# First mixer of an encoder: shifted copies from SBUF to SBUF on two queues, taps of the last tiles spread differently, the gate half normalised first, idle products round the statistics

## The chip, the cores and the metric

The kernel runs on one core of one Trainium2 chip. The metric is the device time of one execution in microseconds (us); the median of several runs counts. Engines are named as in the profile: PE is TensorE (matmuls; PEld its weight loads), DVE is VectorE, ACT is ScalarE, POOL is GpSimd, SP is SyncE, which only issues DMAs here. ACTq and SPq are the DMA queues of ACT and SP.

## The reference, cut to what matters

Two encoder layers on 256 positions of 2048 channels, in float32. Each has a mixer and a feed-forward part with a convolution. The change touches the first mixer alone:

```python
def _conformer_conv(h, w_in, b_in, dw_w, dw_b, ln_g, ln_b, w_out, b_out):
    u = h @ w_in + b_in
    a, gate = jnp.split(u, 2, axis=-1)
    u = a * jax.nn.sigmoid(gate)
    u = _causal_dwconv(u, dw_w, dw_b)
    u = jax.nn.silu(_layernorm(u, ln_g, ln_b))
    return u @ w_out + b_out
```

Here `h` is the RMS norm of the input, `_causal_dwconv` sums 31 shifted copies of a channel with a weight for each (31 taps), and `_layernorm` takes mean and variance over the 2048 channels of a position. The second mixer is an attention, and it, the feed-forward parts and the final norm stay as they are.

## The kernel before

Channels lie on the partitions, 128 at a time, positions along the free axis (S = 256). KT = 16 tiles of 128 channels make up the 2048. Weights come in pieces of 128x1024: SP loads `raw`, ACT rounds it to `hi` (L150), POOL or DVE takes the rest as `lo` (L152), and PE multiplies hi and lo parts. Five raw and six hi and lo buffers go round.

In the first mixer a loop runs over the 16 tiles. Tile i's product with w_in (L229) has 96 matmuls in four steps of 24, in groups of two products with `hi` and one with `lo`; both halves, `a` and gate, stand in one PSUM tile `pp`. `post(i)` then multiplies by the norm's factor `rstd` (L453, DVE), takes the sigmoid `G` of the gate half (L455, ACT) and writes the product into `cpad`, one of three padded tiles (L457, DVE). The convolution of tile i is split in two. Of its 31 taps the first 4·G[i] are done on PE: `u` is written to DRAM (`ud`, L469), read back four times, shifted by one position each time, into the four quarters of a tile `R` (L473, all on ACT's queue), and `taps` multiplies R by diagonals `dg` that POOL builds (L482). A tap product (L498) is 32 columns wide, one of four column groups. G is 3 for tiles 0 to 12 (12 products each), 5 for tile 13 and 6 for tile 14. The other taps are done one after the other on DVE (L536), spread through the steps by `tap_step`. The last tile has no time for copies: 18 taps on PE with full diagonals (`last_taps`, L507; POOL builds them ahead in tiles Y and A, L489) and 13 on DVE in two chains that take turns (L515 to L519).

`dev` adds the bias and takes off a shift `mp`; sums over the tiles of the value and of its square are kept on POOL (L582, L583) and folded into two tiles M at tile 14 (L591). The layernorm sums over the partitions on PE (L286), makes mean and factor in a short chain of DVE and POOL (`mom`, L611 to L617), spreads them over the partitions with four rows products (L292), normalises, and starts w_out (L238, L239).

The order of each engine is set when the kernel is built: a scheduler puts instructions where its own cost model expects their inputs, so a change in one place can move others. `self.at(n, f)` runs `f` n steps later.

Of the kernel before, what the change touches and what calls it, by code (L numbers as in the profile page):

```python
# [8 lines left out]
F32 = mybir.dt.float32  # L9
F32R = mybir.dt.float32r  # L10
AF = mybir.ActivationFunctionType
ALU = mybir.AluOpType
AX = mybir.AxisListType
ET = mybir.EngineType
P = 128
S = 256
EPS = 1e-6
HD = 64
CK = 31
# [6 lines left out]
class Cfg:  # L26


    def __init__(self, d, f, kc=4):
        self.D, self.F = d, f  # L30
        self.KT = d // P
        self.FT = f // P
        self.H = d // (2 * HD)
        self.KC = kc
        self.NW = kc * 256
        self.kcs = [(i, kc) for i in range(0, self.KT, kc)]
        full = self.KT // 2
        first = self.FT % full or full
        self.chunks = [(0, first)] + [(i, full) for i in range(first, self.FT, full)]
        self.VK = kc // 2  # L40
        self.NA, self.NB = self.KT + self.KT // 2 + 1, 8

        self.G = [3] * (self.KT - 3) + [5, 6, 0]

        self.ND = 18

    def dsub(self, ci):
        k0, n = self.chunks[ci]
# [13 lines left out]
class Builder:  # L62
# [379 lines left out]
    def conv_module(self, nin, nout):  # L442
        c, a = self.c, self.a
        nc = self.nc
        KT = c.KT
        D, hh, st = {}, {}, {}
        UW = S + CK + 1

        def post(i, ps):
            with self.tc.high_priority():  # L450

                t = ps[:, :, 0:S]
                nc.vector.tensor_tensor(t, t, nin["rstd"].unsqueeze(1).to_broadcast([P, 2, S]), ALU.mult)  # L453
                sg = self.b1("G")
                nc.scalar.activation(sg, t[:, 1, :], AF.Sigmoid, bias=self.col("bin", KT + i))  # L455
                u = self.cpad[i % 3]
                nc.vector.scalar_tensor_tensor(u[:, CK - 1:CK - 1 + S], t[:, 0, :], self.col("bin", i), sg, ALU.add,  # L457
                                               ALU.mult)
                if i == KT - 1:
                    nc.scalar.activation(self.c2(), sg[:, 0:2], AF.Silu)  # L460
            gm = max(c.G)
            if i == KT - 1:
                self.at(0, lambda: last_taps(u, dgl))
                return

            g = c.G[i]
            n = 4 * (g - 1) + S
            ud = self.dr.tile([P, UW], F32, tag="ud", name=self.nm("ud"), bufs=2)
            nc.scalar.dma_start(ud, u)  # L469
            R = self.ph1.tile([P, 4, 4 * (gm - 1) + S], F32, tag="R", name=self.nm("R"), bufs=2)  # L470
            udv = ud.rearrange("(j c) n -> c j n", j=4)
            for s in range(4):
                nc.scalar.dma_start(R[s * 32:(s + 1) * 32, :, :n], udv[:, :, s:s + n])  # L473
            dg = self.ph1.tile([P, 4 * gm, 32], F32, tag="dg", name=self.nm("dg"))[:, :4 * g, :]

            queue = self.tc.issue_after(self.pool_lo) if i == 0 else ExitStack()
            with queue:
                diagonals(i, g, dg)
            self.at(5 if i < KT - 2 else 4, lambda: taps(i, u, R, dg))

        def diagonals(i, g, dg):
            nc.gpsimd.tensor_tensor(dg, self.cmask.unsqueeze(1).to_broadcast([P, 4 * g, 32]),  # L482
# [10 lines left out]
        def taps(i, u, R, dg):  # L493
            g = c.G[i]
            acc = self.psx("t" if i % 3 == 2 else "s", [P, S])
            for gp in range(g):
                for j in range(4):
                    nc.tensor.matmul(acc[j * 32:(j + 1) * 32, :], dg[:, 4 * gp + j, :], R[:, j, 4 * gp:4 * gp + S],  # L498
                                     start=(gp == 0), stop=(gp == g - 1), tile_position=(0, 32 * j))
            chains.append([i, u, acc, list(range(4 * g, CK))])  # L500

        def last_taps(u, dgl):

            i = KT - 1
            acc = self.psx("s", [P, S])
            for j, w in enumerate(dgl):
                nc.tensor.matmul(acc, w, u[:, j:j + S], start=(j == 0), stop=(j == len(dgl) - 1))  # L507
            while chains:
                tap_step(1000)
            pt = self.pp.tile([P, 2, 512], F32, tag="pp", name=self.nm("pp"))  # L510
            part = [pt[:, x, :S] for x in range(2)]
            for n, j in enumerate(range(len(dgl), CK)):
                w, p = self.col("cw", i * CK + j), part[n % 2]
                if n == 0:
                    nc.vector.scalar_tensor_tensor(p, u[:, j:j + S], w, st["mp"], ALU.mult, ALU.subtract)  # L515
                elif n == 1:
                    nc.vector.tensor_scalar(p, u[:, j:j + S], w, self.col("cb", i), ALU.mult, ALU.add)
                else:
                    nc.vector.scalar_tensor_tensor(p, u[:, j:j + S], w, p, ALU.mult, ALU.add)  # L519
            self.flush()  # L520
            e = self.b1("O")
            nc.scalar.copy(e, acc)
            nc.vector.tensor_tensor(e, part[0], e, ALU.add)
            dev(i, part[1], e)

        dgl = []
        chains = []
# [73 lines left out]
        def layernorm():  # L601
            self.flush()
            while chains:
                tap_step(1000)
                self.flush()
            self.every = None
            self.free(nin["xh"].values())
            mom = self.sm.tile([P, 2, 2], F32, tag="mom", name="mom", bufs=1)
            v, rc, mr = self.c2(), self.c2(), self.c2()
            late = st["late"].rearrange("p (a b) -> p a b", b=2)[:, :, 0]  # L610
            nc.vector.scalar_tensor_tensor(mom.rearrange("p a b -> p (a b)"), late, 1.0 / c.D, st["early"], ALU.mult,  # L611
                                           ALU.add)
            mean, ex2 = mom[:, 0, :], mom[:, 1, :]
            nc.vector.scalar_tensor_tensor(v, mean, -1.0, mean, ALU.mult, ALU.mult)
            nc.vector.scalar_tensor_tensor(v, v, EPS, ex2, ALU.add, ALU.add)
            nc.gpsimd.tensor_tensor(rc, v, self.mhalf, ALU.pow)
            nc.vector.tensor_tensor(mr, mean, rc, ALU.mult)  # L617

            rp = [self.psx("s", [P, S]) for _ in range(2)]
            rs = self.b2("E")  # L620
            for x, v in enumerate((rc, mr)):
                self.rows(rp[x], v)
            pools = [pr for pr in range(2, KT // 2) if pr % 2 == 0]
            ops = (ALU.mult, ALU.subtract)

            def norm(pr, part, j=None):
                d = D[pr][1]
                if j is not None:
                    nc.vector.tensor_tensor(d[:, j, :], d[:, j, :], rp[part], ops[part])
                elif pr in pools:  # L630
                    nc.gpsimd.tensor_tensor(d, d, rs[:, part, :].unsqueeze(1).to_broadcast([P, 2, S]), ops[part])
                else:
                    nc.vector.tensor_tensor(d, d, rp[part].unsqueeze(1).to_broadcast([P, 2, S]), ops[part])

            def act(i):
                z = self.psx("to"[i % 2], [P, S])
                nc.scalar.activation(z, D[i // 2][1][:, i % 2, :], AF.Silu, scale=self.col("lng", i),
                                     bias=self.col("lnb", i))
                hh[i] = self.act_tile()
                nc.scalar.copy(hh[i][1][:, 0, :], z)  # L640
                return z

            def low(i, z):
                h = hh[i][1]
                nc.vector.tensor_tensor(h[:, 1, :], z, h[:, 0, :].bitcast(F32), ALU.subtract)  # L645

            with self.tc.manual_schedule(engines={ET.DVE, ET.Activation, ET.Pool}):
                for j in range(2):
                    norm(0, 0, j)
                    norm(0, 1, j)  # L650
                for x in range(2):
                    nc.scalar.copy(rs[:, x, :], rp[x])
                for pr in pools:
                    norm(pr, 0)
                    norm(pr, 1)
                todo = [(pr, part) for pr in range(1, KT // 2) if pr not in pools for part in range(2)]
                for i in range(KT):
                    z = act(i)
                    for _ in range(2 if i == 1 else 1 if i > 1 else 0):
                        if todo:  # L660
                            norm(*todo.pop(0))
                    low(i, z)
            self.free(D.values())
            self.free([st["sd"]])
# [403 lines left out]
```

## Time and profile before

| | us |
|---|---|
| median of 3 runs | 2267.56 |
| lowest and highest run | 2267.46, 2270.97 |
| the profiled execution | 2268.81 |
| its span in the trace | 2267.0 |
| PE busy | 2219.3 |
| DVE busy | 1635.4 |
| ACT busy | 1205.2 |
| POOL busy | 292.0 |

All times of rows are from the one profiled execution, from the start of its span. The first mixer ends at about 270 us. A time behind an arrow in brackets is the idle time of the engine before the row, and what ended it. A group "x24" is 24 records; a tap product and a ones product have two records each.

### The profile page before, as it was taken

Reading aid. Unit: us, or ns where it says so; the run is one execution under the profiler, and the core shown is the slowest. Engines: PE = TensorE matmul, PEld = TensorE weight load, DVE = VectorE, ACT = ScalarE, POOL = GpSimd, SP = SyncE. Lnnn points to the kernel's source line nnn. Section 1 sums busy time; section 2 is a strip of 40 time slices with the busy share of each in tenths; the row PEclk is TensorE's granted clock in tenths of the full one; section 3 lists DMA queues with packets and bytes.
Section 4 is the critical chain, followed back from the end, with each engine's and each line's share of the span. In section 5 each row is a group of like instructions: output and inputs, shape, how many; then the busy total and the mean of one; then the engine's idle time right before and its main releaser. Section 6 shows DMA issues by size and latency. Waiting matters only on the chain.

```text
span 2267.0 us, 34768 instructions
## 1 busy us (share of the span) xinstructions
PE 2219.3 (98%) x13382; PEld 1944.0 (86%) x13382; DVE 1635.4 (72%) x2491; ACT 1205.2 (53%) x1788; POOL 292.0 (13%) x197
## 2 busy tenths in 40 slices
PE   5999899999999999999999999999999999999998
PEld 5999788788888888888888888888888888888887
DVE  4788675877767777677777677767777677676774
ACT  4333554655545555555555555555555455554554
POOL 4788510100000000000110101110000000000002
PEclk8999999999999999999999999999999999999999
DMA  6677357755555555555555545455555555555552
GB/s 234 196 215 212 116 192 161 241 185 193 187 191 188 187 186 189 191 187 186 195 167 167 167 161 168 151 196 185 189 186 187 192 187 187 191 187 188 188 189 98
DMA packets 126007, 417.55 MB, mean 184 GB/s; under 512 B 14416, under 2 KB 26704, under 8 KB 125840
## 3 DMA queue, kind: packets, MB, share of 16 engines
q1 hardware_dynamic: 113040, 400.42, 53.9%
q10 hardware_dynamic: 11520, 11.45, 2.0%
q0 software_dynamic: 1280, 3.46, 1.3%
q8 instruction: 105, 1.72, 0.3%
q14 instruction: 62, 0.51, 0.1%
HBM read 407.55 MB, written 7.72 MB: 183 GB/s over the span
## 4 chain that ended last, share of the span: by engine, by line
PE 94%; DMA 2%; DVE 1%; POOL 0%; ACT 0%; issue 0%; ACTq 0%; POOLq 0%; DVEq 0%
PE pp L238 48%; PE pp L239 25%; PE pp L229 7%; PE pp L236 4%; PE pp L235 2%; PE pp L807 1%; PE pp L809 1%; PE pp L808 1%; DMA raw<-in_w_up_dram 1%; PE s L498 1%; DMA R<-ud 0%; PE o L292 0%; PE s L854 0%; DMA ud<-cpad 0%; PE t L498 0%; PE o L286 0%
## 5 line engine op out<-in xcount | busy, mean ns | idle before, releaser
L238 PE MATMUL pp<-act,hi 128*128 128x512 f32 x3902 | 1382.6, 396 | 6.2 <-DVE act L645 3.1
L239 PE MATMUL pp<-act,lo 128*128 128x256 f32 x3902 | 1097.5, 281 | 0.0
L150 ACT CAST hi<-raw 128x1024 fp32r<-128x1024 f32 x752 | 788.0, 1049 | 529.2 <-PE pp L238 180.9
L152 DVE TENSOR_TENSOR lo<-raw,hi 128x1024 fp32r<-128x1024 f32 x686 | 846.0, 1234 | 301.0 <-ACT hi L150 299.0
L238 PEld LDWEIGHTS pp<-act,hi 128*128 128x128 f32 x3902 | 733.8, 188 | 167.4 <-DVE act L645 3.4
L239 PEld LDWEIGHTS pp<-act,lo 128*128 128x128 f32 x3902 | 741.1, 190 | 10.3
L238 PE MATMUL pp<-actb,hi 128*128 128x512 f32 x856 | 306.8, 396 | 1.7 <-ACT hi L150 1.7
L239 PE MATMUL pp<-actb,lo 128*128 128x256 f32 x856 | 240.8, 281 | 0.8 <-DVE lo L152 0.8
L333 POOL TENSOR_TENSOR ssq<-ssq,Z 128x512 f32<-128x512 f32 x24 | 35.6, 1483 | 1516.6 <-ACT Z L329 1516.5
L229 PE MATMUL pp<-act,hi 128*128 128x256 f32 x1088 | 203.4, 289 | 9.1 <-ACT act L279 6.2
L238 PEld LDWEIGHTS pp<-actb,hi 128*128 128x128 f32 x856 | 160.7, 188 | 40.1 <-ACT hi L150 2.0
L229 PEld LDWEIGHTS pp<-act,hi 128*128 128x128 f32 x1088 | 173.7, 196 | 15.6 <-ACT act L279 6.2
L152 POOL TENSOR_TENSOR lo<-raw,hi 128x1024 fp32r<-128x1024 f32 x66 | 158.3, 2414 | 57.6 <-ACT hi L150 52.1
L239 PEld LDWEIGHTS pp<-actb,lo 128*128 128x128 f32 x856 | 162.0, 189 | 1.3 <-DVE lo L152 1.1
L229 PE MATMUL pp<-act,lo 128*128 128x256 f32 x544 | 156.5, 288 | 1.7 <-POOL lo L152 1.5
L382 ACT COPY E<-pp 128x512 f32<-128x512 f32 x109 | 63.9, 586 | 171.5 <-PE pp L236 163.8
L268 DVE TENSOR_TENSOR E<-pp,E 128x512 f32<-128x512 f32 x104 | 71.8, 691 | 105.1 <-ACT E L266 104.9
L266 ACT COPY E<-pp 128x512 f32<-128x512 f32 x104 | 60.8, 585 | 162.7 <-PE pp L236 162.5
L704 DVE SCALAR_TENSOR_TENSOR Y<-fpad,prm,Y 128x256 f32<-128x256 f32 x352 | 146.8, 477 | 0.0
L384 DVE TENSOR_TENSOR x<-pp,x 128x512 f32<-128x512 f32 x101 | 69.7, 690 | 89.5 <-ACT E L382 89.0
L701 ACT ACTIVATE Y<-fpad,prm 128x256 f32<-128x256 f32 x176 | 96.3, 595 | 47.5 <-DVE fpad L697 47.5
L229 PEld LDWEIGHTS pp<-act,lo 128*128 128x128 f32 x544 | 106.7, 196 | 2.1 <-POOL lo L152 1.7
(222 smaller groups left out, 1841.9 us busy)
## 6 DMA issues: line engine op xcount, KB each, us to landing
raw<-in_w_up_dram SPq DMA_DIRECT2D x352, 512.0 KB, 3.9
raw<-in_w_down_dram SPq DMA_DIRECT2D x176, 512.0 KB, 3.9
raw<-in_w_in_dram SPq DMA_DIRECT2D x64, 512.0 KB, 4.4
raw<-in_w_qk_dram SPq DMA_DIRECT2D x64, 512.0 KB, 3.6
raw<-in_w_out_dram SPq DMA_DIRECT2D x32, 512.0 KB, 3.9
raw<-in_w_v_dram SPq DMA_DIRECT2D x32, 512.0 KB, 3.6
raw<-in_w_o_dram SPq DMA_DIRECT2D x32, 512.0 KB, 3.6
R<-ud ACTq DMA_DIRECT2D x52, 132.0 KB, 4.6
```

The costliest lines, as they stand in the source:

```text
L150: nc.scalar.copy(hi[:, :n], raw[:, :n])
L152: ins = eng.tensor_tensor(lo[:, :n], raw[:, :n], hi[:, :n].bitcast(F32), ALU.subtract)
L229: nc.tensor.matmul(ps[:, 0:S], w[:, kk, cs], xt[:, x, :], start=(k == first and n == 0), stop=(k == last and n == 2))
L236: nc.tensor.matmul(*main, start=False, stop=True)
L238: nc.tensor.matmul(*main, start=(k == first), stop=False)
L239: nc.tensor.matmul(*corr, start=False, stop=False)
L266: nc.scalar.copy(cs, ps[:, :, S:])
L268: nc.vector.tensor_tensor(t, ps[:, :, 0:S], cs, ALU.add)
L382: nc.scalar.copy(cs, ps[:, :, S:])
L384: nc.vector.tensor_tensor(x, ps[:, :, 0:S], x, ALU.add)
L701: nc.scalar.activation(y[:, j, :], u[:, j, FK - 1:], AF.Identity, scale=self.col("fw", ch * FK + FK - 1), bias=self.col("fb", ch))
L704: nc.vector.scalar_tensor_tensor(y[:, j, :], u[:, j, q:q + S], self.col("fw", ch * FK + q), y[:, j, :], ALU.mult, ALU.add)
```

## The change

The copies of `u` into R go from SBUF to SBUF with no DRAM tile between: sixteen DMAs of 32 partitions for each tile, eight on SP's queue and eight on ACT's, instead of one write and four reads on ACT's. Of tile 14's taps, the seven of DVE no longer stand in the common chain: `few_taps` computes them into a tile of their own one step after `post`, and `taps` of tile 14 comes one step earlier. The last tile has 16 taps on PE instead of 18, so no A diagonals, and 15 on DVE. Tile 15's gate half is multiplied by `rstd` ahead of the other half. In the layernorm PE gets idle products (ones by ones, 128x128, nobody reads the result): seven ahead of the rows products and eight behind them.

```diff
-        self.ND = 18
+        self.ND = 16
...
-                nc.vector.tensor_tensor(t, t, nin["rstd"].unsqueeze(1).to_broadcast([P, 2, S]), ALU.mult)
+                if i < KT - 1:
+                    nc.vector.tensor_tensor(t, t, nin["rstd"].unsqueeze(1).to_broadcast([P, 2, S]), ALU.mult)
+                else:
+                    for x in (1, 0):
+                        nc.vector.tensor_tensor(t[:, x, :], t[:, x, :], nin["rstd"], ALU.mult)
...
-            ud = self.dr.tile([P, UW], F32, tag="ud", name=self.nm("ud"), bufs=2)
-            nc.scalar.dma_start(ud, u)
             R = self.ph1.tile([P, 4, 4 * (gm - 1) + S], F32, tag="R", name=self.nm("R"), bufs=2)
-            udv = ud.rearrange("(j c) n -> c j n", j=4)
-            for s in range(4):
-                nc.scalar.dma_start(R[s * 32:(s + 1) * 32, :, :n], udv[:, :, s:s + n])
+            for j in range(4):
+                for s in range(4):
+                    (nc.sync if s < 2 else nc.scalar).dma_start(R[s * 32:(s + 1) * 32, j, :n], u[j * 32:(j + 1) * 32, s:s + n])
...
-            self.at(5 if i < KT - 2 else 4, lambda: taps(i, u, R, dg))
+            if i == KT - 2:
+                self.at(1, lambda: few_taps(i, u))
+            self.at(5 if i < KT - 2 else 3, lambda: taps(i, u, R, dg))
...
-            chains.append([i, u, acc, list(range(4 * g, CK))])
+            if i < KT - 2:
+                chains.append([i, u, acc, list(range(4 * g, CK))])
+            else:
+                self.at(1, lambda: dev(i, acc, part14[0]))
+
+        part14 = []
+
+        def few_taps(i, u):
+
+            p = self.psx("o", [P, S])
+            for n, j in enumerate(range(4 * c.G[i], CK)):
+                w = self.col("cw", i * CK + j)
+                if n == 0:
+                    nc.vector.scalar_tensor_tensor(p, u[:, j:j + S], w, st["mp"], ALU.mult, ALU.subtract)
+                else:
+                    nc.vector.scalar_tensor_tensor(p, u[:, j:j + S], w, p, ALU.mult, ALU.add)
+            e = self.b1("O")
+            nc.scalar.activation(e, p, AF.Identity, bias=self.col("cb", i))
+            part14.append(e)
...
             e = self.b1("O")
-            nc.scalar.copy(e, acc)
-            nc.vector.tensor_tensor(e, part[0], e, ALU.add)
-            dev(i, part[1], e)
+            nc.scalar.copy(e, part[0])
+            nc.vector.tensor_tensor(e, part[1], e, ALU.add)
+            dev(i, acc, e)
...
+            idle = self.pp.tile([P, 2, 512], F32, tag="pp", name=self.nm("pp"))
+
+            def keep_warm(n):
+                for _ in range(n):
+                    i = nc.tensor.matmul(idle[:, 0, :P], self.ones, self.ones, start=True, stop=True)
+                    self.tc.keep_in_program_order(i)
+
+            keep_warm(7)
             mom = self.sm.tile([P, 2, 2], F32, tag="mom", name="mom", bufs=1)
...
                 self.rows(rp[x], v)
+            keep_warm(8)
```

The scheduler also moves other instructions. On PE, in the middle of tile 10's product (`pp`), where its first step gives way to the second, stand the taps of tile 8 (into `t`). Before:

```order
L229 MATMUL pp_1892<-act_138,hi_1720 128x256 x2
L229 MATMUL pp_1892<-act_138,lo_1721 128x256
L498 MATMUL t_1917<-R_1711,dg_1716 32x256 x12
L229 MATMUL pp_1892<-act_145,hi_1772 128x256 x2
L229 MATMUL pp_1892<-act_145,lo_1773 128x256
```

On PE, the same place after the change:

```order
L229 MATMUL pp_1990<-act_138,hi_1808 128x256 x2
L229 MATMUL pp_1990<-act_138,lo_1809 128x256
L502 MATMUL t_2015<-R_1787,dg_1804 32x256
L229 MATMUL pp_1990<-act_145,hi_1860 128x256 x2
L502 MATMUL t_2015<-R_1787,dg_1804 32x256 x9
L229 MATMUL pp_1990<-act_145,lo_1861 128x256
```

The twelve tap products stood in one run; now nine do, and three stand alone ahead of it among the w_in products, one of them here and two further up.

On ACT, round the sigmoid of an early tile (`G`: G_681 is tile 2's before; G_699 is tile 2's and G_883 tile 3's after the change), with the casts of the weights and the copies. Before:

```order
L150 CAST hi_615<-raw_454 128x1024
L150 CAST hi_651<-raw_484 128x1024
L150 CAST hi_695<-raw_527 128x1024
L150 CAST hi_747<-raw_577 128x1024
L455 ACTIVATE G_681<-pp_533,prm 128x256
L469 DMA ud_684<-cpad_258 128x288
L150 CAST hi_789<-raw_613 128x1024
L473 DMA R_686<-ud_684 32x4x264 x4
```

On ACT after the change (hi_723 is the first weight piece of tile 4's product):

```order
L459 ACTIVATE G_699<-pp_551,prm 128x256
L475 DMA R_526<-cpad_255 32x264 x3
L150 CAST hi_633<-raw_462 128x1024
L150 CAST hi_669<-raw_492 128x1024
L475 DMA R_702<-cpad_258 32x264 x8
L459 ACTIVATE G_883<-pp_727,prm 128x256
L150 CAST hi_723<-raw_545 128x1024
L570 ACTIVATE M_765<-s_576,prm 128x256
L150 CAST hi_775<-raw_595 128x1024
```

Casts that stood ahead of a sigmoid now stand behind it, and behind copies.

On POOL, the end of the mixer (`lo` pieces, the sums L582 and L583, the folds M). Before:

```order
L152 TENSOR_TENSOR lo_2868<-raw_2691,hi_2867 128x1024
L152 TENSOR_TENSOR lo_3116<-raw_2735,hi_3115 128x1024
L582 TENSOR_TENSOR act_914<-act_914,act_2787 128x512
L583 TENSOR_TENSOR lnsq<-lnsq,Z_2861 128x512
L152 TENSOR_TENSOR lo_3139<-raw_2795,hi_3138 128x1024
L591 TENSOR_TENSOR M_2971<-act_914 128x256
L591 TENSOR_TENSOR M_2972<-lnsq 128x256
```

On POOL after the change, whose last `lo` pieces are the ninth and those before it from tile 14's sigmoid on:

```order
L152 TENSOR_TENSOR lo_2956<-raw_2757,hi_2955 128x1024
L152 TENSOR_TENSOR lo_2991<-raw_2793,hi_2990 128x1024
L152 TENSOR_TENSOR lo_3051<-raw_2829,hi_3050 128x1024
L613 TENSOR_TENSOR M_3083<-act_952 128x256
L605 TENSOR_TENSOR lnsq<-lnsq,Z_3044 128x512
L152 TENSOR_TENSOR lo_3284<-raw_2883,hi_3283 128x1024
L152 TENSOR_TENSOR lo_3307<-raw_2953,hi_3306 128x1024
L613 TENSOR_TENSOR M_3084<-lnsq 128x256
```

The second fold stands behind two more `lo` pieces, and the sum of squares behind the first fold.

## Rows read from the trace of the kernel before

**Rows 1.** the page, busy time of an engine, share of the span, instructions
```profile
PE 2219.3 (98%) x13382; PEld 1944.0 (86%) x13382; DVE 1635.4 (72%) x2491; ACT 1205.2 (53%) x1788; POOL 292.0 (13%) x197
```

**Rows 2.** the chain of waits, 176 to 200 us: start, length, what
```profile
177.41 1.43 PE s L498 x24
178.84 11.71 PE pp L229 x96
```

**Rows 3.** PE's timeline, taps of tiles 12 and 13 among w_in products
```profile
216.55 0.28 PE L229 MATMUL pp<-act,lo 128*128 128x256 f32 x1
216.76 1.50 PE L498 MATMUL s<-R,dg 128*32 128x256 f32 x24
...
218.53 0.29 PE L229 MATMUL pp<-act,lo 128*128 128x256 f32 x1
...
229.69 0.28 PE L229 MATMUL pp<-act,lo 128*128 128x256 f32 x1
229.90 2.37 PE L498 MATMUL s<-R,dg 128*32 128x256 f32 x40
...
232.53 0.28 PE L229 MATMUL pp<-act,lo 128*128 128x256 f32 x1
```

**Rows 4.** PE's timeline, the ones product among w_in products
```profile
80.05 0.28 PE L229 MATMUL pp<-act,lo 128*128 128x256 f32 x1
80.17 0.59 PE L556 MATMUL o<-M,ones 128*128 128x256 f32 x2
...
80.83 0.28 PE L229 MATMUL pp<-act,lo 128*128 128x256 f32 x1
```

**Rows 5.** PE's timeline, tile 0's taps
```profile
61.54 1.50 PE L498 MATMUL s<-R,dg 128*32 128x256 f32 x24 [1.16 <-DMA R<-ud]
```

**Rows 6.** PE's timeline, rows products and the first w_out product
```profile
257.36 1.66 PE L292 MATMUL s<-ident,c 128*128 128x128 f32 x8 [1.52 <-POOL c L616]
262.11 0.80 PE L238 MATMUL pp<-act,hi 128*128 128x512 f32 x1 [3.09 <-DVE act L645]
```

**Rows 7.** POOL's timeline
```profile
35.69 0.61 POOL L489 TENSOR_TENSOR A<-ident,cprm 128x256 f32<-128x256 f32 x1
...
224.25 9.47 POOL L152 TENSOR_TENSOR lo<-raw,hi 128x1024 fp32r<-128x1024 f32 x4
...
241.64 1.28 POOL L582 TENSOR_TENSOR act<-act,act 128x512 f32<-128x512 f32 x1
...
247.30 0.72 POOL L591 TENSOR_TENSOR M<-lnsq 128x256 f32<-128x256 f32 x1
```

**Rows 8.** the tile R, its DMAs
```profile
DMA to landing us min/median/max: 2.4/4.7/7.2
```

**Rows 9.** timelines of DVE and ACT, from tile 14's normalisation to mom
```profile
227.13 0.70 DVE L453 TENSOR_TENSOR pp<-pp,rstd 128x512 f32<-128x512 f32 x1 [0.96 <-PE pp L229]
...
228.00 0.47 ACT L455 ACTIVATE G<-pp,prm 128x256 f32<-128x256 f32 x1
...
233.87 1.77 ACTq L473 DMA_DIRECT2D R<-ud  x4
...
254.24 0.42 DVE L569 TENSOR_TENSOR act<-pp,O 128x256 f32<-128x256 f32 x1
255.95 0.16 DVE L611 SCALAR_TENSOR_TENSOR mom<-o,early 128x4 f32<-128x4 f32 x1 [1.29 <-PE o L286]
```

**Rows 10.** groups by line, 56 to 262 us: busy, mean ns, idle before
```profile
L150 ACT CAST hi<-raw 128x1024 fp32r<-128x1024 f32 x56 | 58.5, 1048 | 117.2 <-PE pp L229 54.5 <-DMA R<-ud 31.4 <-POOL dg L482 11.3
```

**Rows 11.** windows of 2 us: busy (x) of PE, PEld, DVE, ACT, POOL; PEclk; DMA
```profile
256.00:258.00 2.00, 0.64 (x5) 0.64 (x6) 0.66 (x5) 0.00 (x0) 0.72 (x1) 0.96 0.00 0
258.00:260.00 2.00, 1.02 (x5) 0.72 (x4) 1.33 (x4) 0.11 (x1) 0.00 (x0) 0.50 0.00 0
266.00:268.00 2.00, 2.00 (x8) 1.71 (x7) 2.00 (x5) 1.94 (x6) 1.92 (x2) 0.50 0.00 0
268.00:270.00 2.00, 2.00 (x13) 1.78 (x12) 1.47 (x4) 1.39 (x4) 0.16 (x1) 0.98 0.01 4
```

## The prediction

> **What bounds the kernel now.** I read the page first: TensorE (PE) is busy for 98% of the span [rows 1]. So an operation added on PE costs its own length unless PE was idle there, and work taken from another engine is worth only the PE idle time that it ended. The change lies in the first mixer, up to about 270 us. There the chain of waits shows the rhythm of a tile: 96 products of w_in in 11.71 us, 0.122 each, then one run of tap products [rows 2]. No step of another engine stands in that part of the chain. The timeline of PE then gives prices: what a run of tap products adds between two w_in products [rows 3], and what a single full-precision product adds [rows 4]. Last I looked for places where PE does stand: before tile 0's taps (1.16 us, for a DMA into R) [rows 5] and round the layernorm, where the first rows product waits for POOL and the first w_out product 3.09 us for DVE [rows 6].
>
> **The price of a tap product, and of a run.** The run of tile 12 is 12 products in three rounds of four column groups (24 records); from the lo product before it to the one behind it 218.53 − 216.55 = 1.98 us pass. One step of the usual rhythm is three products, 0.36, so the run adds 1.62. Tile 13's run of 20, in five rounds, adds 232.53 − 229.69 − 0.36 = 2.48 [rows 3]. Two rounds more cost 0.86, so a round is 0.43 and each run has 0.33 besides, whatever its length. Check: 96 × 0.122 + 1.62 = 13.3, and the chain has 1.43 + 11.71 = 13.1 for a tile [rows 2].
>
> **Lone tap products: +23.6.** The order of PE after the change splits the taps. Each tile of 0 to 12 keeps a main run of 9 to 11 products, and one to three products are issued before it in short runs of their own, among w_in products; up to the end of tile 14's product I count 44 runs where there were 13, so 31 more, 28 of them a single product and 3 of two or three. A short run fills one round at most. It takes what a round takes, 0.43, and the fixed 0.33 of a run: 0.76. The main run keeps three rounds, since the fullest column group still has three products, so nothing is given back. 31 × 0.76 = 23.6. No row shows a 32-column product alone, so I bound it. From below, the nearest row is the ones product: lo to lo 80.83 − 80.05 − 0.36 = 0.42 [rows 4], hence 31 × 0.42 = 13.0. Nearer to none, as if it ran beside the w_in products, is a rival below. From above, 0.76. I take the upper one, because the fixed part appears in both tap runs that I measured and not at the ones product, which has the width of its neighbours.
>
> The 0.33 per run and the ones product's 0.42, the same as one round without it, suggest that going from 128 columns to 32 and back is what costs. The Trainium skill, "TensorEngine Tiling (Array Packing)", section Tiling Modes (Key Properties), says that changing the tiling mode, not just the tile, drains TensorE. By that rule every lone product would pay two such changes and the sum above would stand; without it the term would be 13.0.
>
> **Gone at the start: −0.6 and −1.2.** ND goes from 18 to 16, so the A diagonals (0.61 on POOL) no longer stand ahead of the lo pieces and rc [rows 7]: −0.6, or 0 if rc waits for something else. Tile 0's copies no longer go through DRAM; the PE wait of 1.16 before its taps [rows 5] goes, unless the sixteen copies take as long: R's copies land 2.4 to 7.2 us after issue [rows 8], and ACT needs 0.44 to issue one (four in 1.77) [rows 9]. Eight issues are 3.5; with the median landing of 4.7 that is 8.2, near what two transfers one after the other take. I take −1.2, at worst 0.
>
> **ACT's order at tile 4: +2.8, and the copies of tile 3: +1.0.** Before, ACT's casts run four ahead of a tile's sigmoid. After, the first cast of tile 4's weights stands behind tile 3's sigmoid, and that waits for tile 3's last product and the normalisation. From the norm's start to the sigmoid 228.00 − 227.13 = 0.87, the sigmoid 0.47 [rows 9], the cast 1.05 [rows 10], and some 0.2 from product to norm: 2.6 after the product's end. PE has only tile 2's taps, 1.62, to bridge: it stands 1.0. Its third product then needs the lo piece, which POOL makes in 9.47/4 = 2.37 [rows 7], while PE has two products (0.24) and a ones product (0.42): 1.8 more. Together 2.8; 0 if the scheduler's order leaves time that I do not see. Tile 3's eight copies on ACT stand behind four casts: 4 × 1.05 + 3.5 + 2.4 landing = 10.1 us after the sigmoid, of a tile of 13.1, while lone products of these taps are due ahead of their main run. I take 1.0, with 0 to 4 as bounds.
>
> **The end, from tile 14's sigmoid (228.00, called G): 0.0 (−2.9 to +3.1).** Before, POOL's last sum M<-lnsq ends at 247.30 + 0.72, G + 20.0, and mom on DVE starts at 255.95, G + 28.0, 1.71 after the last add of tile 15's deviation starts [rows 7, 9]: DVE's tap chain was last. After, POOL has nine lo pieces, two sums of 1.28 and two of 0.72 from the cast behind G on: G + 0.47 + 1.05 + 9 × 2.37 + 2.56 + 1.44 = G + 26.9. With the same 1.71 behind it mom is at G + 28.6: +0.6. DVE's chain gets shorter (tile 14's taps, which alternated with it, have their own place earlier), but that is worth nothing once POOL is last; so are the gate half first and the wait before tile 14's taps. Seven idle products then stand ahead of the rows products. The four rows products (8 records) take 1.66 [rows 6], 0.41 each, at a granted clock of 0.50, the 1.2 GHz level, and the clock is 0.96 to 258 us [rows 11]: seven idle products take 1.5 at the full 2.4 GHz and 2.9 at half. Before, the rows products started 257.36 − 255.95 = 1.41 behind mom, so +0.1 to +1.5: +0.8. Eight more stand behind, 1.7 to 3.3, in a gap that is 4.75 from rows to w_out with 1.66 of it used: +0.1. In return the clock: from 262.11 on the w_out products run at 0.50 until 268 (0.98 from there) [rows 6, 11]; if PE kept the full level, these 5.9 us would be 2.95, a gain of up to 2.9. I take half, −1.5, since PE still has an idle stretch before w_out. +0.6 + 0.8 + 0.1 − 1.5 = 0.0.
>
> **Sum.** 23.6 − 0.6 − 1.2 + 2.8 + 1.0 + 0.0 = +25.6. The profiled execution took 2268.8, 1.2 above the median of the runs, so against the median 2293.
>
> On the copies: the Trainium skill, "DMA: Bandwidth & Descriptors", Rules for kernel authors, says that spreading DMAs over several issuers adds no bandwidth, since all run on the same 16 engines, and saves only issue time. By it, sixteen small copies among raw weight loads would not land faster than four large ones did; that is the case of late copies below.
>
> **Rivals.**
> Lone products at 0.42 each: a full-precision product and no fixed part. For it, the ones product; against it, the width does change. 13.0 + 2.0 = +15.0: 2282.6.
> Copies late: sixteen DMAs per tile wait on SP behind raw loads whose buffers come free late, and PE stands at lone products which come earlier than the run did. For it, landing up to 7.2 [rows 8]; against it, the taps have had some 13 us. A quarter of a microsecond at half of the 44 runs and 4 at tile 3 would make about +10: 2303.
> Not slower: a lone product hides beside the w_in products, as one column group does beside another (a quarter round, 0.11, taken out of the main run). Then the 31 runs cost nothing, the rest is +2.0: 2269.6, no change. It decides below 2.5/31 = 0.08 per lone product. Against it stands the 0.33 that no run escaped.
> Faster: that, tile 4's wait and tile 3's copies hidden (−3.8), the whole clock gain (−1.4 more) and the idle products at the full clock (−0.7): 2.0 − 5.9 = −3.9, 2263.7. Even all of them only come to the edge of 0.2%.
> The redistribution does nothing: earlier taps of tile 14, ND, and the gate half only move what ends before POOL's last sum; that is inside my forecast.
>
> **How the numbers follow.** A run of this kernel tells from no change about 0.2%, 4.5 us. Forecast 0.58 (its own range 2287 to 2299), lone products at 0.42: 0.17, copies late: 0.14, not slower: 0.08, faster: 0.03. The likeliest is 2293. The low end takes the second case with the terms at their low bounds (13.0 − 0.6 − 1.2 − 2.9 + 2.8 = 11.1): 2278.6, so 2278; the high end lies past the late copies, 2306. Slower 0.89, same 0.08, faster 0.03.
>
> **What would show it.** Lone records of the tap line among w_in products, with lo-to-lo distances of 1.1 us instead of 0.36 (0.78 in the second case); a tile of about 15 us instead of 13.1; PE idle at the first product of tile 4 for ACT's cast; rc about 0.6 earlier; POOL's M<-lnsq ending last before mom; rows at 0.5 or 1.0 clock behind the idle products. Everything behind the first mixer should be shifted, not changed. I am wrong if tiles still last 13.1, or if PE waits for R at many places.

## The result, and the profile after

The changed kernel takes 2296.62 us (median of 4 runs, 2296.17 to 2299.18), the kernel before 2267.86 (4 runs): a ratio of 1.0126 with a 95% interval of 1.0109 to 1.0144. It is 29 us slower. The forecast was 2293, with 2278 to 2306 for its range.

The page of the changed kernel, against [rows 1]: the span is 28.1 longer and PE is busy for 29.0 more, with 26 more records: 30 of the fifteen idle products, less 4 of the two diagonals that went.

```profile
span 2295.1 us, 35125 instructions
...
PE 2248.3 (98%) x13408; PEld 1953.1 (85%) x13408; DVE 1638.2 (71%) x2494; ACT 1202.7 (52%) x1789; POOL 290.8 (13%) x196
```

Four marks cut the 28.1 into pieces: tile 14's sigmoid G, mom, the first w_out product, the end of the span.

| piece | before | after | difference | forecast |
|---|---|---|---|---|
| to tile 14's sigmoid | 228.00 | 251.88 | +23.9 | +25.6 |
| sigmoid to mom | 27.95 | 32.93 | +5.0 | +0.6 |
| mom to the first w_out product | 6.16 | 7.55 | +1.4 | +0.9 |
| first w_out product to the end | 2004.89 | 2002.74 | −2.15 | −1.5 |

**The short runs.** PE's timeline of the changed kernel, round a single tap product (two records) among w_in products; to be read against [rows 3, 4]:

```profile
58.09 0.28 PE L229 MATMUL pp<-act,lo 128*128 128x256 f32 x1
58.21 0.28 PE L229 MATMUL pp<-act,hi 128*128 128x256 f32 x1
58.42 0.62 PE L502 MATMUL s<-R,dg 128*32 128x256 f32 x2
58.97 0.38 PE L229 MATMUL pp<-act,hi 128*128 128x256 f32 x1
59.19 0.28 PE L229 MATMUL pp<-act,lo 128*128 128x256 f32 x1
```

From lo to lo 59.19 − 58.09 = 1.10 us pass where a step takes 0.36, so the short run costs 0.74; the forecast had 0.76. The reader is to see that the tap record starts 0.21 behind the record ahead of it, and that the next w_in product starts 0.55 behind it: in between no w_in product starts. Measured from the start of the record ahead of a run to that of the second one behind it, less two usual distances (0.24), every short run in the trace costs 0.74 or 0.75, those of two and three products too, and the main runs of 9 and 10 still cost 1.60 to 1.61, as the runs of 12 did before (1.62). 31 × 0.74 = 22.9.

**Tile 4.** PE's timeline where tile 4's product begins:

```profile
84.99 1.50 PE L502 MATMUL t<-R,dg 128*32 128x256 f32 x22
87.29 0.50 PE L229 MATMUL pp<-act,hi 128*128 128x256 f32 x2 [0.81 <-ACT hi L150]
87.67 0.70 PE L578 MATMUL o<-M,ones 128*128 128x256 f32 x2
89.73 0.39 PE L229 MATMUL pp<-act,lo 128*128 128x256 f32 x1 [1.36 <-POOL lo L152]
```

The run of tile 2's taps ends, PE waits 0.81 for ACT's cast, does two products and the ones product, and waits 1.36 for POOL's lo piece: 2.2 for the 2.8 that were forecast. The wait of 1.16 before tile 0's taps [rows 5] is gone. 22.9 + 2.2 − 1.2 and the 0.5 by which rc comes earlier make 23.4 of the 23.9. The 1.0 for tile 3's late copies is not there: no wait of PE in the mixer is for R.

**The end.** ACT's timeline of the changed kernel, from tile 14's sigmoid:

```profile
251.88 0.47 ACT L459 ACTIVATE G<-pp,prm 128x256 f32<-128x256 f32 x1 [11.83 <-DVE pp L454]
252.25 1.99 ACT L150 CAST hi<-raw 128x1024 fp32r<-128x1024 f32 x2
253.71 0.52 ACTq L475 DMA_DIRECT2D R<-cpad  x1
254.13 1.05 ACT L150 CAST hi<-raw 128x1024 fp32r<-128x1024 f32 x1
254.26 7.34 ACTq L475 DMA_DIRECT2D R<-cpad  x7
261.70 1.05 ACT L150 CAST hi<-raw 128x1024 fp32r<-128x1024 f32 x1 [6.52 <-DMA R<-cpad]
```

and POOL's, which waits for these casts:

```profile
253.37 7.27 POOL L152 TENSOR_TENSOR lo<-raw,hi 128x1024 fp32r<-128x1024 f32 x3 [5.75 <-ACT hi L150]
262.83 2.41 POOL L152 TENSOR_TENSOR lo<-raw,hi 128x1024 fp32r<-128x1024 f32 x1 [2.19 <-ACT hi L150]
...
280.32 0.71 POOL L613 TENSOR_TENSOR M<-lnsq 128x256 f32<-128x256 f32 x1
```

The casts go on behind the sigmoid, then the eight copies of R take ACT's queue for 7.9 us, and the fourth cast comes only at 261.70, behind the copies. POOL's lo piece starts 2.19 late at 262.83, and its last fold ends at 280.32 + 0.71 = 281.03, G + 29.2 instead of the forecast G + 26.9. DVE adds the last part to it (`M<-M,O`). PE sums the result over the partitions (L286), ACT scales the sums into `early`, and mom on DVE follows:

```profile
281.07 0.43 DVE L614 TENSOR_TENSOR M<-M,O 128x256 f32<-128x256 f32 x1 [2.38 <-POOL M L613]
...
282.60 0.17 ACT L617 ACTIVATE early<-o 128x4 f32<-128x4 f32 x1 [3.46 <-PE o L286]
...
284.81 0.16 DVE L642 SCALAR_TENSOR_TENSOR mom<-o,early 128x4 f32<-128x4 f32 x1 [3.32 <-PE o L286]
```

PE has nothing to do meanwhile. Its timeline shows the wait, the sums, the idle products (L635), the rows products (L292), and w_out:

```profile
281.55 1.02 PE L286 MATMUL o<-ones,M 128*128 128x2 f32 x4 [4.98 <-DVE M L614]
282.83 1.02 PE L286 MATMUL o<-ones,act 128*128 128x2 f32 x4 [0.26 <-ACT early L617]
283.70 0.99 PE L286 MATMUL o<-ones,O 128*128 128x2 f32 x4
284.56 3.33 PE L635 MATMUL pp<-ones 128*128 128x128 f32 x14
287.68 1.55 PE L292 MATMUL s<-ident,c 128*128 128x128 f32 x8
289.07 1.95 PE L635 MATMUL pp<-ones 128*128 128x128 f32 x16
292.36 0.50 PE L238 MATMUL pp<-act,hi 128*128 128x512 f32 x1 [1.34 <-DVE act L677]
```

and windows of 2 us the clock, as in [rows 11]:

```profile
278.00:280.00 2.00, 0.00 (x0) 0.00 (x0) 0.58 (x2) 0.42 (x1) 2.00 (x2) 0.62 0.45 127
280.00:282.00 2.00, 0.45 (x3) 0.46 (x3) 0.43 (x1) 0.00 (x0) 1.70 (x3) 0.50 0.66 182
290.00:292.00 2.00, 1.02 (x10) 0.83 (x8) 0.60 (x3) 1.74 (x5) 1.32 (x2) 1.00 0.00 0
292.00:294.00 2.00, 1.64 (x8) 1.22 (x8) 1.97 (x5) 1.03 (x3) 2.00 (x2) 1.00 0.01 4
```

PE waits 4.98 us, its granted clock goes to 0.50 (the 1.2 GHz level) while it waits, and the sums, the seven idle products and most of the rows products run before it is back. From POOL's fold to mom 3.8 us pass instead of the 1.71 that were forecast. Before, the last sums ran at the full clock:

```profile
254.81 0.58 PE L286 MATMUL o<-ones,act 128*128 128x2 f32 x4 [0.78 <-DVE act L569]
255.25 0.59 PE L286 MATMUL o<-ones,O 128*128 128x2 f32 x4
```

These two groups took 1.03 us then (254.81 to 255.84) and take 1.86 now (282.83 to 284.69). The rest of the difference is a longer way: before, the sums of M and `early` were done ahead of the last add; now both stand behind the fold, 1.33 us from the end of DVE's add (281.50) to the sums of `act` (282.83). At 290 us the clock is 1.00 and w_out starts at it, where before it started at 0.50.

### The profile page after: what moved, and what is told of

It is laid out like the page before. It is cut to its first block, busy times and chain, and to the rows that moved or that the text cites. A ratio compares the mean times of both kernels' runs of the same rounds, so it can differ in the third digit from the quotient of the medians.

```text
span 2295.1 us, 35125 instructions
## 1 busy us (share of the span) xinstructions
PE 2248.3 (98%) x13408; PEld 1953.1 (85%) x13408; DVE 1638.2 (71%) x2494; ACT 1202.7 (52%) x1789; POOL 290.8 (13%) x196
## 4 chain that ended last, share of the span: by engine, by line
PE 94%; DMA 2%; POOL 1%; DVE 1%; issue 1%; ACT 0%; POOLq 0%; SPq 0%; DVEq 0%; ACTq 0%
PE pp L238 47%; PE pp L239 24%; PE pp L229 7%; PE pp L236 4%; PE pp L235 2%; PE pp L839 1%; PE pp L841 1%; PE pp L840 1%; DMA raw<-in_w_up_dram 1%; PE s L502 1%; POOL lo L152 1%; DMA raw<-in_w_in_dram 0%; PE o L286 0%; PE o L292 0%; PE t L502 0%
```

## The experiments

Ratios are to the kernel before on the same chip. Theory A is the forecast: a short run costs 0.74 on PE, wherever it stands.

**Split alone** (e6_split_alone). The kernel before; the first tap product of tiles 1 to 12 is issued one step earlier, and the products of a tile's taps are pinned in their order (the functions that do it are left out here):

```diff
-            self.at(5 if i < KT - 2 else 4, lambda: taps(i, u, R, dg))
+            if 0 < i < KT - 3:
+                self.at(4, lambda: first_tap(i, R, dg))
+            self.at(5 if i < KT - 2 else 4, lambda: taps(i, u, R, dg))
```

> The kernel before, with the copies through DRAM and every other engine's order as it was; only PE changes: of the taps of tiles 1 to 12 the first product is issued alone, 24 w_in products ahead of the other eleven. Twelve short runs more than before. Theory A (a short run costs a round and the fixed part of a run, measured 0.74 us in the changed kernel from lo product to lo product): 12 x 0.74 = +8.9 us, 2276.8. Theory B (the split costs little by itself, about 0.1 a product, and the time went into waits round the new copies): +1 at most, 2268 to 2269.

Measured: 1.0045 (1.0029 to 1.0060), 10.2 us by the ratio. PE's timeline of it, round one such product:

```profile
136.45 0.28 PE L229 MATMUL pp<-act,lo 128*128 128x256 f32 x1
136.66 0.62 PE L502 MATMUL s<-R,dg 128*32 128x256 f32 x2
137.21 0.51 PE L229 MATMUL pp<-act,hi 128*128 128x256 f32 x2
137.55 0.28 PE L229 MATMUL pp<-act,lo 128*128 128x256 f32 x1
```

137.55 − 136.45 − 0.36 = 0.74 again, and the sigmoids of neighbouring tiles, 13.14 us apart before, stand 13.87 apart: 12 × 0.73 = 8.8 us, as theory A has it. The copies are as before, and the orders of ACT, POOL, DVE and SP differ only in the places of a few casts, lo pieces and diagonals. One thing more differs in this trace: PE's two waits for R, 1.2 and 1.4 before, are gone. So the price of a short run is shown in the steady tiles, without the new copies. Theory B falls for this term.

**One run in the changed kernel** (e1_one_run). The products of a tile's taps are pinned one behind the other, and the column group whose copies are issued last comes first (arguments cut):

```diff
-                for j in range(4):
-                    nc.tensor.matmul(...)
+                for j in (3, 2, 1, 0):
+                    m = nc.tensor.matmul(...)
+                    self.tc.keep_in_program_order(m)
```

> The changed kernel with the taps of a tile held together in one run on PE; copies, redistribution and idle products stay. Theory A (33 short runs at 0.74): 24.4 us less than the changed kernel, about 2272; the 4 to 5 us that are left are the order of ACT at tile 4 and the late sum on POOL at the end. Theory B (waits round the copies): most of the loss stays, about 2290, since the copies and ACT's order stay.

Measured: 1.0073 (1.0059 to 1.0088). It is 0.53% better than the changed kernel (the quotient of the two ratios), about 12 us: half of what theory A wanted, and more than theory B allowed. Neither holds alone. The trace has 15 runs of taps. Tile 14's sigmoid comes at 237.76, 14.1 earlier than in the changed kernel and not 22.9, and from there to mom 36.5 us pass instead of 32.9. PE's waits from 56 us on (in total, times, longest):

```profile
PE o L286 <- DVE M L615: 4.6, 1, 4.6
PE s L530 <- DVE cpad L461: 3.8, 1, 3.8
PE pp L229 <- POOL lo L152: 3.7, 5, 1.0
PE pp L229 <- ACT hi L150: 2.9, 1, 2.9
```

PE waits for a cast 2.9 and for lo pieces 3.7 at five places, where the changed kernel had 0.8 and 1.4; at tile 4 its clock falls to 0.50 behind the two waits; and it waits 3.8 for the last tile's `cpad`. From these waits I read that the engines that feed PE are the slower ones once the short runs are gone.

**Copies alone** (e2_copies_alone), the kernel before with the sixteen copies, and the same **with one run** (e2b_copies_one_run):

```diff
-            ud = self.dr.tile([P, UW], F32, tag="ud", name=self.nm("ud"), bufs=2)
-            nc.scalar.dma_start(ud, u)
...
+            for j in range(4):
+                for s in range(4):
+                    (nc.sync if s < 2 else nc.scalar).dma_start(R[s * 32:(s + 1) * 32, j, :n], u[j * 32:(j + 1) * 32, s:s + n])
```

> The kernel before with the sixteen copies from SBUF to SBUF on two queues alone; no redistribution of taps, no idle products, gate half not ahead. The scheduler then splits the taps by itself: 49 runs where there were 15. Theory A: 34 x 0.74 = +25, less 1 to 2.6 for the waits for R that go, plus 2.2 at tile 4: about 2292. Theory C (the redistribution at the end is what costs, through POOL's last sum): the copies alone give at most +5, 2273.

> The kernel before with the sixteen copies on two queues alone, and the taps of a tile held in one run. Against the copies with split taps (1.0115), theory A takes off 34 short runs at 0.74, 25 us: 2268. Theory G (short runs make PE slow enough for late casts, raw loads and lo pieces to keep up; without them these waits come out, as they did in the changed kernel with one run, where 12 of 24 us came back): only about half goes, 2280.

Measured: 1.0115 (1.0101 to 1.0130) and 1.0079 (1.0064 to 1.0094). The copies alone bring most of the loss, with no redistribution and no idle products, and the split comes with them: 49 runs instead of 15. The likely reason stands in the code and was not tried by itself: a product of column group j now needs only group j's four copies, so the scheduler can place it by itself. Theory C falls. With one run 0.36% come back, 8 us of the 25. That speaks for theory G and against A, but it is a third and not the half that G expected.

**All copies on one queue**, each with one run a tile (e7_one_run_sp, e8_one_run_act): `(nc.sync if s < 2 else nc.scalar)` becomes `nc.sync`, or `nc.scalar`.

> The changed kernel with one run of taps for a tile, and all sixteen copies on SP's queue; on ACT's the casts stand ahead of the sigmoids again. In the run with eight on each queue 18 us over the kernel before were left. Theory D1 (ACT's issuing of copies holds the casts up, and POOL's lo pieces and last sum with them): most of it goes, 2268 to 2272. Theory D2 (copies that wait for cpad on SP hold the raw weight loads up): it grows, 2290 and more, with ACT's casts waiting for raw loads.

> The changed kernel with one run of taps for a tile, and all sixteen copies on ACT's queue; SP issues raw weight loads alone. Theory D1 (ACT's issuing holds the casts up): 16 x 0.6 = 9.6 us of issuing for a tile of 13.1, beside four casts of 1.05: 2300 and more. Theory D2 (raw loads behind copies on SP): most of the 18 us goes, 2272.

Measured: 1.0096 (1.0083 to 1.0109) on SP and 1.0139 (1.0126 to 1.0152) on ACT. Both are slower than eight on each (1.0073), the first only just beyond the noise. ACT's waits with the copies on SP, and ahead of them the same wait in the kernel before:

```profile
ACT hi L150 <- DMA raw<-in_w_in_dram: 4.6, 1, 4.6
...
ACT hi L150 <- DMA raw<-in_w_in_dram: 108.0, 37, 9.2
```

and on ACT:

```profile
ACT G L459 <- DMA R<-cpad: 58.2, 5, 14.2
```

On SP the casts wait 108 us, at 37 places, for raw weight loads that stand behind copies; before it was 4.6, once. SP's own timeline of that run shows why:

```profile
102.35 12.55 SPq L475 DMA_DIRECT2D R<-cpad  x16
115.00 1.95 SPq L140 DMA_DIRECT2D raw<-in_w_in_dram  x4
```

Sixteen copies and four loads take SP's queue from 102.35 to 116.95, 14.6 us with two short pauses among the copies, and the next sixteen follow at 117.05. The sigmoids of neighbouring tiles stand about 15.2 apart instead of 13.14. The loads are late in being issued, not in being moved: from issue to landing they take 4.7 us at the median, against 4.4 before and 4.5 in the changed kernel. On ACT the sigmoids wait 58 us behind the copies of an earlier tile. D1 and D2 are both true, each of its queue: neither queue has room for the copies.

**The redistribution alone** (e9_redistribution_alone): the changed kernel with the old copies and without `keep_warm`.

> The changed kernel with the old copies through DRAM and without idle products: only the redistribution of the last tiles' taps (16 diagonals, few_taps) and the gate half ahead are left. On every engine the casts stand ahead of the sigmoids again and the taps are in one run each. Theory A: -0.6 for the A diagonals, and at the end the sums on POOL stand where they stood: -0.5 to -2, 2265 to 2267. Rival (redistribution is what puts POOL's last sum late): +3 to +5, 2271.

Measured: 1.0028 (1.0017 to 1.0039), slower. PE's waits in it:

```profile
PE o L286 <- DVE M L616: 3.2, 2, 1.8
...
PE t L504 <- DMA R<-ud: 2.8, 1, 2.8
```

With the slower way through DRAM tile 14's taps, which now come a step earlier, stand ahead of the end of tile 15's product, and PE waits 2.8 for R there and 3.2 for the folds. Theory A was wrong here: the redistribution is no gain without fast copies. The loss, about 6 us by the ratio, is even above the 3 to 5 of the rival.

**Copies only at the ends** (f2_hybrid): the changed kernel with the copies from SBUF for tiles 0 and 14, through DRAM for the others, one run, no idle products (`direct = i == 0 or i == KT - 2`). And the kernel before with them **for tile 0 alone** (f3_tile0_only).

> The changed kernel, but copies from SBUF to SBUF only for tiles 0 and 14, the others through DRAM as before; taps in one run each; no idle products. Theory D (copies in the steady tiles are what holds ACT and SP up; at the two ends they are free): -0.6 for the A diagonals, -1.2 for tile 0's wait, end between -1.5 and +3 with POOL's last sum: 2265 to 2269. Rival (the redistribution at the end costs by itself): 2273 and more.

> The kernel before with copies from SBUF to SBUF for tile 0 alone, taps in one run each. Theory: PE's wait of 1.2 before tile 0's taps goes, nothing else: 0.9995, not to be told from no change. Rival (the eight copies on SP hold raw loads up even once): +1 to +3.

Measured: 1.0015 (1.0006 to 1.0024) and 1.0001 (0.9993 to 1.0010). The steady tiles of f2 are 13.14 us apart again and tile 14's sigmoid is at 225.59, 2.4 earlier than before; the end gives more than that back, at the fold (from that sigmoid to mom 33.5 us, where it was 27.95):

```profile
PE o L286 <- DVE M L623: 5.8, 1, 5.8
```

Here it is not POOL that is late: its last fold ends at 252.17, but DVE's add behind it comes only at 255.38, after the last tile's tap chain. So the copies in the steady tiles cost, and the end costs by itself. f3 shows no difference; the 1.2 of tile 0 is below what the runs can tell. No version beats the kernel before.

**The folds on DVE** (e5_one_run_fold_dve), with one run: `nc.gpsimd.tensor_tensor(h[x], ...)` becomes `nc.vector.tensor_tensor`.

> The changed kernel with one run of taps for a tile, and the two folds M at tile 14 on DVE (0.4 us each) instead of POOL, where the second stands behind lo pieces. In the run without this PE waited 4.6 us for the last fold. Theory F (that fold's place on POOL is the end's wait): 3 to 5 us less, 2281 to 2283. Rival (the sum of squares that it folds is itself late on POOL): 1.5 less at most.

Measured: 1.0082 (1.0069 to 1.0095), not better than without (1.0073). Theory F falls. In its trace the two folds take 2.55 and 1.45 us on DVE and the two adds behind them 2.56 and 2.17, where an add of that size took 0.42 before [rows 9], all of it in the middle of the last tile's tap chain. The timelines of POOL and DVE, at the last of them, show what stands beside it:

```profile
262.99 7.32 POOL L152 TENSOR_TENSOR lo<-raw,hi 128x1024 fp32r<-128x1024 f32 x3
268.42 2.17 DVE L615 TENSOR_TENSOR M<-M,O 128x256 f32<-128x256 f32 x1
```

The add starts beside POOL's third lo piece and ends at 270.59, 0.28 us after that piece (270.31). Each of the other three also ends 0.28 or 0.29 after the POOL piece beside which it started, and so does the add of 2.57 us in e9 (253.96, with the lo piece ending at 253.68). The taps of the chain, which add to a PSUM tile, take 0.48 each beside the same pieces. So these adds, whose tiles all lie in SBUF, stood until POOL's piece was done; that reading comes from the times alone, no run tried it.

**The idle products**, added alone to the kernel before (e3_idle_alone) and taken out of the changed one (e4_no_idle):

> The kernel before with the fifteen idle products round the layernorm's statistics alone. Theory A: the first seven run at the 1.2 GHz level or the 2.4 GHz level, so rows products are 0.1 to 1.5 us later; the first w_out products run at the full clock and give 2 to 2.9 back: net -0.5 to -2.8, 2265 to 2267. Rival: the clock is at its lower level all the same when w_out begins, so only the delay is left: +0.1 to +1.6.

> The changed kernel without its fifteen idle products. In the kernel before, adding them alone gave 0.9999. Theory A: the seven ahead of the rows products cost 1.5 and the full clock at w_out gave back 2 to 2.7: without them +0.5 to +1.2 against the changed kernel, 2297 to 2298. Rival (idle products are part of the loss): 2 us or more less, 2294.

Measured: 0.9999 (0.9990 to 1.0008), and 1.0126 (1.0110 to 1.0142), the same as with them; a difference of 2 us would lie within these intervals. PE's timeline of e3 [rows 6]:

```profile
255.66 2.98 PE L612 MATMUL pp<-ones 128*128 128x128 f32 x13
...
263.44 0.50 PE L238 MATMUL pp<-act,hi 128*128 128x512 f32 x1 [1.06 <-DVE act L654]
```

In e3 mom is at 255.56; the first w_out product comes 7.88 behind it instead of 6.16, 1.7 later, and starts at the full rate; from it to the end 2002.6 pass instead of 2004.9, 2.3 less. In the changed kernel, against e4, mom to w_out takes 7.55 instead of 6.59 and the rest 2002.74 instead of 2003.78, so about 1.0 each way. Within what the runs can tell, cost and gain cancel.

## Why the prediction was right, step by step

**Lone tap products** (forecast +23.6): the term that decides, and its price was right, 0.74 for 0.76, in the changed kernel and in e6. Its premise that a main run keeps three rounds held too (1.60 to 1.61). The rival at 0.42 and the one in which a lone product hides both fall. The sentence of the Trainium skill ("TensorEngine Tiling (Array Packing)", Tiling Modes, Key Properties) that a change of the tiling mode drains TensorE agrees with it: 0.74 less a round of 0.43 leaves 0.31 for two changes; what the engine does in that time no run shows.

**What the prediction did not see**: the term stands in the sum of this kernel, but it is not what the change would save if the split were mended. Taking it away gave 12 of 24 us (e1) and 8 of 25 (e2b). Copies hold up the raw loads where they stand on SP and the sigmoids and casts where they stand on ACT (e7, e8); that the slower PE covered this in the changed kernel is read from PE's waits in e1. I had this only as waits at tile 4 and tile 3.

**Start**: rc 0.5 earlier for 0.6, tile 0's wait gone, as forecast. **Tile 4**: 2.2 for 2.8, by the two waits that were named (the second was put at 1.8, though 2.37 less 0.66 is 1.7; it measured 1.36). **Tile 3's copies**: 0 for 1.0; PE does not wait for R in e1 either, where no short runs slow it.

**The end** (0.0, with −2.9 to +3.1): measured +5.0 + 1.4 − 2.15 = +4.3, outside its bounds. That POOL's last fold would end last was right. Two sizes were off. I gave the eight copies no time on ACT in front of the cast that follows; they took 7.9 us. And I carried 1.71 from the last add to mom over to the fold, and it was 3.8. The 1.71 was measured with PE at its full clock, and behind a wait of 5 us it ran at half; and it held one add and the last sums, while behind the fold the sums of M and `early` stand in between. The net of idle products and clock, −0.6 in the forecast, is −0.75 in these pieces (1.4 − 2.15), and e3 and e4 show no difference in time.

**Luck in the total**: the trace has +28.1 where the terms gave +25.6. The end missed by 4.3, and the short runs, tile 4 and tile 3 together fell 2.3 short of their terms, so part of the misses cancelled.

**Issuing a copy** was taken at the 0.44 of [rows 9]. In the changed kernel the copies of R take (durations in ns, then issue to landing in us):

```profile
L475 SPq DMA_DIRECT2D R<-cpad x120: 507/584/1716, 52.2 to 263.7; - x120
L475 ACTq DMA_DIRECT2D R<-cpad x120: 514/602/1902, 52.2 to 261.1; - x120
...
DMA to landing us min/median/max: 1.7/3.3/5.9
```

240 issues at a median of 0.58 and 0.60, sixteen for a tile, about 9.5 us of two queues in 13.1; before, it was five on one. Landing is faster, 3.3 at the median for 4.7 [rows 8], so late copies were not the loss. The rule of the Trainium skill ("DMA: Bandwidth & Descriptors", Rules for kernel authors), that several issuers only save issue time, put the weight on the right thing, the issue time; here the small copies cost more of it than the second queue saves. Its other half, that several issuers add no bandwidth, no run here tests: these copies land faster, but they are also smaller and leave out DRAM.

What stays open: why an issue that is 0.51 at best takes up to 1.9, and how much of the time that e1 did not win back lies in each wait, since they follow from each other.

## What to carry to other kernels

Price a scheduler's new order row by row: a 32-column product issued alone costs a whole round and the change of shape, some six times its share in a run of twenty (2.48/20 = 0.12). When a transfer is cut into many small ones, count the issues on each queue and ask what stands behind them; and where two engines are nearly in step, expect that mending the one shows the other.

## What the runs showed that was not expected

Fifteen idle products of 128x128 bring PE back to its full clock before w_out, and the time they take on the way is about what the clock gives back: 1.7 against 2.3 us in the kernel before, 1.0 against 1.0 in the changed one. The time of the kernel is the same with and without them. And moving the folds from POOL to DVE, off the engine that was late, made nothing faster: there they and the adds behind them took three to six times what such an add takes elsewhere, and each ended just after the piece of POOL's work beside which it had started.
